# The second gate of a hybrid block: three of four pairs of output units as seven half-width block products

## The chip, the cores and the metric

The kernel runs on one core of a Trainium2 chip, as one launch. The metric is the device time of that launch in microseconds (us); the times given are medians of runs, and one further execution was recorded by the hardware profiler. TensorE is called PE below (PEld is its weight load), VectorE DVE, ScalarE ACT, GpSimd POOL and SyncE SP. SP and POOL here issue the DMAs: SP plain ones, POOL those that add to what the destination holds.

## The reference, cut to what matters

One decoder block on 512 tokens of 1024 channels, in float32. `h` is the normalised, shifted and scaled input. The part around the change is the merge of two branches by two sigmoid gates:

```python
proj = h @ w_in
z, xbc, dt_raw, u_pool, gate_logits = jnp.split(proj, IN_SPLITS, axis=-1)
...
y_ssd = y.reshape(b, seq, D_INNER) @ w_branch_ssd
y_pool = causal_multiscale_pool(u_pool, pool_w, pool_scale) @ w_branch_pool
g_ssd, g_pool = jnp.split(jax.nn.sigmoid(gate_logits), N_BRANCHES, axis=-1)
return (g_ssd * y_ssd + g_pool * y_pool) @ w_out
```

The gate of the SSD branch, `g_ssd`, is the "second gate": a 512 x 1024 by 1024 x 1024 product, then a sigmoid. The block ends with an MLP of width 4096 with a squared ReLU and a last norm.

## The kernel before, in words

All activations are kept transposed: channels on the 128 partitions, the 512 tokens along the free axis. A matrix product is cut into **units** of 128 output channels: `unit` (line 160) takes a packed weight of 128 x 1024 (eight blocks of 128 x 128, one for each 128 input channels) and accumulates into one PSUM bank of 128 x 512. To keep float32 accuracy, each operand is held as a rounded high part and a low rest, and `mm3` (line 154) issues three matmuls for each block: high by high, high by low, low by high. So a unit is 8 x 3 = 24 matmuls of 512 columns.

`load_unit` (line 136) brings the weight into one of four raw buffers (`RAW`) by a DMA on SP, rounds it on ACT (line 146), and takes the rest on DVE (line 147) into two of the `HL` buffers. `split` (line 123) does the same with an activation (lines 126 and 127). Buffers come from `Slots`, a first-in-first-out list of tiles: a tile's next user waits for all readers of its last one. `ada` (line 168) loads a row of the modulation weights into a raw buffer as well and reduces it on DVE (line 172); 32 of these rows are spread over the middle of the kernel by `ada_next`. The instructions of each engine are put in order by the framework when the program is built, by priority and its own estimate of when each is ready; work can be placed well ahead of its position in the program.

The order of the middle of the kernel is: four SSD groups with their fillers; eight units of the gate of the pooling branch (`wgate[8 + j]`, line 700); inside it, after the fourth, the last part of the SSD branch product (`bs`) and a mix of the pool; eight units of the pool projection (`wbp`, line 718), which multiply into `merged` (line 720), with two `ada` each; the eight units of the second gate (`wgate[j]`, line 725): sigmoid on ACT (line 728), times the SSD branch `acc` (line 730), plus `merged` (line 731), and `split`, giving `mg`; then the output projection (`wout`, line 784), whose every unit reads all eight `mg`. The second gate also issues the last four `ada`.

The MLP already uses another form, for **pairs** of output units (class `Pair`, line 877). The contraction's eight blocks are taken as four even-odd couples, the pair's two units and the two halves of the tokens are the other two splits, so that the product is a 2 x 2 by 2 x 2 block product, done with seven block products in place of eight (Winograd's form of Strassen's scheme). `product` (line 871) is one of these: four blocks by three matmuls of 256 columns, so a pair is 7 x 12 = 84 matmuls of 256 columns. The sums it needs:

- of the moving operand, `sums` (line 841): four operations of 256 columns on DVE for each of four couples, and two splits (`two`, line 835);
- of the weights, S1 to S4 beside A11, A12 and A22: two by accumulating DMAs on POOL (lines 892 and 894), two by DVE (lines 908 and 919), and the splits by `keep` (lines 896 to 901, with the rounding and the rest at lines 837 and 839);
- of the products: two copies on ACT (lines 961 and 968), two additions on DVE (lines 973 and 980).

`run_jobs` (line 996) runs a list of jobs, pairs or plain ones: it fetches the weights of those ahead as raw buffers come free (`pump`), prepares the next job between the products of the present one, and leaves the last two products of a pair to the time of the next job, so that PE does not wait for DVE:

```python
self.mul(self.ac[:, :H], "A11", "B11", True)   # first
self.mul(self.c12, "S1", "T1", True)           # open
self.mul(self.ac[:, :H], "S2", "T2")           # middle
self.mul(self.c11, "A12", "B21")
self.mul(self.ac[:, :H], "S3", "T3")           # third
self.mul(self.c12, "S4", "B22")                # close
self.mul(self.ac[:, :H], "A22", "T4")          # finish
```

PSUM has eight banks of 128 x 512: a pair uses a set of two of banks 4 to 7 (`BE`), and one of banks 0 and 1 (`AC`); banks 2 and 3 are left for plain units.

Of the kernel before, what the change touches and what calls it, by code (L numbers as in the profile page):

```python
# [12 lines left out]
P = 128  # L13
# [49 lines left out]
def block_kernel(tc, xp, crow, arow, par, adaT, wstart, wz, wx, wpool_in, wgate, wpw, wbs, wbp, wout, wup, wdn, out):  # L63
# [3 lines left out]
    with (  # L67
# [616 lines left out]

        urgent[0] = True
# [6 lines left out]
        PADS = slots("pad", 9, (P, T + 16))  # L692
        pu = [pool_in(gi, t) for gi in range(4) for t in range(2)]
        rest = run(3, after(2, pu[:6] + [pool_mix(0)] + pu[6:]))
        later = [p_.get() for p_ in (XS, SZ, XS)]
        F = Slots(lambda i, dt: later[i // 4][:, i % 4, :], 12)


        merged = []
        for j in range(8):  # L700
# [5 lines left out]
            if j == 1:  # L706
                for _ in rest:
                    pass
                later.append(SZ.get())
                F.free += range(12, 16)  # L710
                PU.free += PS.free
            ada_next()
            if j == 3:
# [3 lines left out]
                pool_mix(1)()  # L717
        for j in range(8):
# [3 lines left out]
            ada_next(2)  # L722
        free(pout)
        mg = []
        for j in range(8):
            gs = F.get()
            ps = unit(wgate[j], h)
            last = act.activation(gs, ps, AF.Sigmoid)
            PU.put(ps)
            dve.tensor_tensor(gs, gs, acc[j], ALU.mult)  # L730
            dve.tensor_tensor(gs, gs, merged[j], ALU.add)
            S.put(acc[j])
            F.put(merged[j])
            mg.append(split(gs))
            F.put(gs)
            if rows:
                ada_next()
# [90 lines left out]
        HL = Slots(lambda i, dt: D(B0 + i if i < 8 else B0 + 9, dt, 48), 9)  # L828
# [4 lines left out]
        Y4S = Slots(lambda i, dt: slots("pad", 1, (P, T + 16), first=APART[i][0]).get(dt)[:, APART[i][1]:APART[i][1] + T], 4)  # L833

        def two(src, dst, late=None):

            act.copy(dst[0], src)  # L837
            with tc.issue_after(late.ins) if late else nullcontext():
                dve.tensor_tensor(dst[1], src, dst[0].bitcast(F32), ALU.subtract)  # L839

        def sums(u1, u2, ts):

            dve.tensor_tensor(u1[:, :H], u1[:, :H], u1[:, H:], ALU.subtract)
            dve.tensor_tensor(u1[:, H:], u2[:, H:], u1[:, H:], ALU.subtract)
# [32 lines left out]
        class Pair:  # L877
# [79 lines left out]
            def open(self):  # L957
                self.take()
                self.mul(self.c12, "S1", "T1", True)
                with tc.high_priority():  # L960
                    act.copy(self.s5, self.c12)
# [370 lines left out]
```

## Time and profile before

| what | value |
|---|---|
| median of three runs | 957.82 us (955.89 to 960.07) |
| the profiled execution | 958.36 us |
| its span, first to last instruction | 956.6 us |
| mean granted clock of PE over the span | 0.995 |
| matmul groups of 512 columns, three products (lines 156 to 158) | 920 each, of these 112 with 256 columns (operands `s` and `d`) |
| half-width matmuls of pairs (line 875) | 1848, in 22 pairs |

A row of the busy time by stretch reads: the stretch in us from the start of the span, its length, and then for each engine the us in which it was busy and the number of instructions. In a timeline a row reads: start, duration, engine, line, operation, the tiles written and read, the shape, a count, and in brackets how long the engine stood idle before it and what released it. Matmuls are pipelined: their durations overlap, and what one costs is the spacing of their starts.

### The profile page before, as it was taken

What the parts mean: (1) busy time and instruction counts of PE and PEld (TensorE: products, weight loads), DVE (VectorE), ACT (ScalarE), POOL (GpSimd) and SP (SyncE); (2) the same over time, 40 slices, a digit from 0 to 9 for tenths busy, and PEclk for the clock granted to TensorE, in tenths of its full rate; (3) what the DMA queues carried; (4) which work ended last, traced back from release to release, by engine and by line L of the source; (5) the groups of instructions that cost most, each with busy time, mean ns of one, the idle gap of its engine ahead of it and who ended that gap; (6) DMA issues with size and microseconds to landing.
All of it is one profiled execution on the core that took longest, in us unless ns stands there. A gap on an engine that the chain in (4) does not pass through costs nothing.

```text
span 956.6 us, 14343 instructions
## 1 busy us (share of the span) xinstructions
PE 940.4 (98%) x5491; PEld 810.9 (85%) x5491; DVE 721.3 (75%) x1120; ACT 540.8 (57%) x891; POOL 124.3 (13%) x131
## 2 busy tenths in 40 slices
PE   8999999999999999999999999999999999999996
PEld 4877888888888888787888888998999899899986
DVE  7978868566767776987568565698869888977973
ACT  5479976568436642553421343486458547646753
POOL 0102320220312031410000000001111111111000
PEclk9999999999999999999999999999999999999998
DMA  9836343433354343464578464035676676677412
GB/s 362 310 119 181 118 129 98 136 121 97 88 144 122 99 116 96 158 192 156 181 237 287 152 201 151 29 91 126 159 200 152 151 198 147 165 194 169 133 35 88
DMA packets 70503, 145.55 MB, mean 152 GB/s; under 512 B 5473, under 2 KB 30305, under 8 KB 70434
## 3 DMA queue, kind: packets, MB, share of 16 engines
q1 hardware_dynamic: 64672, 134.14, 44.5%
q0 software_dynamic: 5760, 10.49, 7.4%
q8 instruction: 43, 0.70, 0.3%
q14 instruction: 26, 0.21, 0.1%
q10 hardware_dynamic: 2, 0.00, 0.0%
HBM read 142.39 MB, written 2.23 MB: 151 GB/s over the span
## 4 chain that ended last, share of the span: by engine, by line
PE 75%; DVE 12%; DMA 5%; ACT 4%; issue 2%; POOL 0%; SPq 0%; DVEq 0%; POOLq 0%; ACTq 0%
PE ps L875 18%; PE ps L156 16%; PE ps L157 16%; PE ps L158 16%; PE ps L328 4%; DMA d<-wdn 3%; DVE d L839 2%; DVE d L147 1%; PE ps L549 1%; DMA d<-cs_d 1%; DVE s L127 1%; DVE s L839 1%; ACT d L837 1%; PE ps L529 1%; DMA d<-wstart 1%
## 5 line engine op out<-in xcount | busy, mean ns | idle before, releaser
L156 PE MATMUL ps<-s,d 128*128 128x512 f32 (+1 forms) x920 | 350.6, 381 | 1.1 <-ACT s L649 0.6
L157 PE MATMUL ps<-s,d 128*128 128x512 f32 (+1 forms) x920 | 345.9, 376 | 0.2 <-DVE s L127 0.2
L158 PE MATMUL ps<-s,d 128*128 128x512 f32 (+1 forms) x920 | 346.0, 376 | 0.0
L156 PEld LDWEIGHTS ps<-s,d 128*128 128x128 f32 x920 | 172.6, 188 | 35.7 <-issue 2.1
L158 PEld LDWEIGHTS ps<-s,d 128*128 128x128 f32 x920 | 172.8, 188 | 32.4 <-issue 0.2
L157 PEld LDWEIGHTS ps<-s,d 128*128 128x128 f32 x920 | 172.8, 188 | 31.2 <-DVE s L127 0.7
L875 PE MATMUL ps<-s,d 128*128 128x256 f32 x1314 | 162.2, 279 | 2.1 <-DVE d L839 2.0
L875 PEld LDWEIGHTS ps<-s,d 128*128 128x128 f32 x1314 | 156.9, 188 | 4.2 <-DVE d L839 3.8
L147 DVE TENSOR_TENSOR d<-d,d 128x1024 fp32r<-128x1024 f32 x88 | 112.6, 1280 | 63.1 <-ACT d L146 56.6
L146 ACT CAST d<-d 128x1024 fp32r<-128x1024 f32 x88 | 92.0, 1046 | 117.8 <-PE ps L157 77.2
L837 ACT CAST d<-d 128x1024 fp32r<-128x1024 f32 x86 | 89.8, 1048 | 56.9 <-DVE d L919 24.1
L839 DVE TENSOR_TENSOR d<-d,d 128x1024 fp32r<-128x1024 f32 x86 | 104.7, 1221 | 18.9 <-ACT d L837 10.2
L172 DVE CUSTOM_DVE_ANT_0 d<-d,d,par_t 128x1024 f32<-128x1024 f32 x32 | 41.8, 1306 | 27.3 <-DMA d<-adaT 27.1
L892 POOL DMA_DIRECT2D d<-wdn x10 | 8.8, 884 | 307.5 <-DMA d<-wdn 258.7
L328 PE MATMUL ps<-s,d 128*128 128x512 f32 x168 | 41.7, 403 | 1.9 <-ACT s L316 1.9
L499 ACT ACTIVATE d<-d,ncs 128x128 f32<-128x128 f32 x128 | 39.9, 390 | 3.9 <-POOL d L495 3.8
L328 PEld LDWEIGHTS ps<-s,d 128*128 128x128 f32 x168 | 32.5, 194 | 10.0 <-ACT s L316 2.4
L397 DVE SCALAR_TENSOR_TENSOR s<-ps,par_t,s 128x511 f32<-128x511 f32 (+2 forms) x54 | 39.6, 741 | 0.3
L126 ACT CAST s<-s 128x512 fp32r<-128x512 f32 x32 | 19.7, 619 | 31.1 <-POOL s L511 18.7
L495 POOL TENSOR_SCALAR_AFFINE_SELECT d<-d 128x1024 f32<-128x1024 f32 x16 | 18.2, 1137 | 90.8 <-ACT cd L492 37.0
L127 DVE TENSOR_TENSOR s<-s,s 128x512 fp32r<-128x512 f32 x32 | 25.7, 805 | 4.4 <-ACT s L126 4.3
L511 POOL TENSOR_TENSOR s<-s,dec 128x512 f32<-128x512 f32 x12 | 15.8, 1313 | 90.7 <-issue 56.4
(231 smaller groups left out, 1231.6 us busy)
## 6 DMA issues: line engine op xcount, KB each, us to landing
d<-adaT SPq DMA_DIRECT2D x32, 512.0 KB, 4.2
d<-wup SPq DMA_DIRECT2D x32, 512.0 KB, 4.8
d<-wdn SPq DMA_DIRECT2D x32, 512.0 KB, 4.6
d<-wx SPq DMA_DIRECT2D x18, 512.0 KB, 3.6
d<-cs_d SPq DMA_DIRECT2D x16, 512.0 KB, 6.0
d<-wbs SPq DMA_DIRECT2D x16, 512.0 KB, 3.6
d<-wgate SPq DMA_DIRECT2D x16, 512.0 KB, 4.2
d<-wz SPq DMA_DIRECT2D x15, 512.0 KB, 3.6
```

Of the source, the lines that this page charges most:

```text
L146: act.copy(hi[:, :w], r[:, a:a + w])
L147: (low or dve).tensor_tensor(lo[:, :w], r[:, a:a + w], hi[:, :w].bitcast(F32), ALU.subtract)
L156: pe.matmul(ps, whi, xhi[:, t0:t1], start=start, stop=False)
L157: pe.matmul(ps, whi, xlo[:, t0:t1], start=False, stop=False)
L158: pe.matmul(ps, wlo, xhi[:, t0:t1], start=False, stop=stop)
L172: dve.tensor_tensor_reduce(r, r, cbc, 1.0, col("b_ada", j), ALU.mult, ALU.add, mod[:, j:j + 1])
L328: pe.matmul(first[u], w[u][i // 2], h[k][i % 2], start=k == 0 and i == 0, stop=k == 7 and i == 2)
L397: dve.scalar_tensor_tensor(t[:, sh:], ps[:, :T - sh], w(3 - sh), t[:, sh:], ALU.mult, ALU.add)
L499: act.activation(m[:, i, :], m[:, i, :], AF.Exp, bias=ncs[:, c, g * HG + i:g * HG + i + 1])
L837: act.copy(dst[0], src)
L839: dve.tensor_tensor(dst[1], src, dst[0].bitcast(F32), ALU.subtract)
L875: pe.matmul(ps, x, y, start=start and m == 0 and i == 0, stop=m == 3 and i == 2, skip_group_check=True)
```

## The change

The second gate's first six units become three pairs; its last two stay plain units.

- The weights are packed once more, as pairs (`wgs`).
- `whole(m)` restores the float32 values of two couples' blocks of `h` by adding its two parts on DVE, makes the four sums T1 to T4 of them and splits these. It is called at the last two units of the pooling gate and at units 1 and 3 of `wbp`. The sums of the first two couples lie where gate buffers of the merge were, those of the other two in eight `S` slots.
- `gate_pair` applies the sigmoid to the pair's results and calls `merge`, the old sequence of product, sum and split.
- Classes and helpers of the MLP's pairs move ahead of the gate stage, unchanged but for their buffers: in the gate stage, the pairs' raw buffers are `RAW`, their splits come from `HL`, which is eleven buffers long by then (eight before).
- The first pair is fetched and wholly prepared at unit 4 of `wbp`; `run_jobs` becomes a generator that stops there and goes on after `wbp`. The fetches of the other two pairs stand behind the last `wbp` unit in the program.
- The last four `ada` are issued by the two plain units (two each) in place of the first four units of the gate.
- In the gate stage plain units have PSUM banks 2 and 3 only.

```diff
+        def whole(m):
+
+            us = [S.get(), S.get()]
+            for u, (hi, lo) in zip(us, h[2 * m:2 * m + 2]):
+                dve.tensor_tensor(u, hi.bitcast(F32), lo.bitcast(F32), ALU.add)
+            if m < 2:
+                ts = [tuple(later[2 + m][:, 2 * i + a, :].bitcast(F32R) for a in range(2)) for i in range(2)]
+            else:
+                ts = [(S.get(F32R), S.get(F32R)) for _ in range(2)]
+            sums(*us, ts)
+            S.put(*us)
+            return ts
+
+        def merge(j, gs):
+
+            dve.tensor_tensor(gs, gs, acc[j], ALU.mult)
+            dve.tensor_tensor(gs, gs, merged[j], ALU.add)
+            S.put(acc[j])
+            F.put(merged[j])
+            mg.append(split(gs))
+            S.put(gs)
+
+        def gate_pair(p):
+
+            def f(i, ps, sign):
+                gs = S.get()
+                n = T // len(ps)
+                for i_, part in enumerate(ps):
+                    act.activation(gs[:, n * i_:n * (i_ + 1)], part, AF.Sigmoid, scale=float(sign))
+                merge(2 * p + i, gs)
+            return Pair(wgs[p], hb, f)
...
+            def run(self, between):
+                for j in range(2 * NPAIR, 8):
+                    ps = unit(wgate[j], h)
+                    if between:
+                        between()
+                        between = None
+                    gs = S.get()
+                    self.last = act.activation(gs, ps, AF.Sigmoid)
+                    PU.put(ps)
+                    merge(j, gs)
+                    while len(rows) > 2 * (7 - j):
+                        ada_next()
...
+            if j > 5:
+                ht.append(whole(j - 6))
+        mg, hb = [], {}
+        for j in range(8):
+            ps = unit(wbp[j], pout)
+            dve.tensor_tensor(merged[j], merged[j], ps, ALU.mult)
+            PU.put(ps)
+            ada_next(2)
+            if j in (1, 3):
+                ht.append(whole(len(ht)))
+            if j == 4:
...
+                RL, Z = RAW, HL
+                HP = Slots(lambda i, dt: D(NRAW + i, dt, 48), 11)
+                HP.free = HL.free
+                hb.update(moving(h, ht))
+                gates = [gate_pair(p) for p in range(NPAIR)] + [GateUnits()]
+                steps = run_jobs(gates)
+                next(steps)
+        free(pout)
+        banks, BE, AC = banks_of_pairs()
+        PU.free = [2, 3]
+        for _ in steps:
+            pass
```

In `run_jobs`, ahead of the loop over the jobs:

```diff
-            pump()
-            jobs[0].prepare()
+            if isinstance(jobs[0], Pair):
+                todo.pop(0).fetch()
+                jobs[0].prepare()
+                jobs[0].prepare_more()
+                jobs[0].prepare_rest()
+            else:
+                pump()
+                jobs[0].prepare()
+            yield
             pump()
```

More of the change, by code (lines that the diff above doesn't have):

```diff
@@ L60, in put, with block_kernel @@
             self.free.append(self.owner.pop(id(t))[0])
-def block_kernel(tc, xp, crow, arow, par, adaT, wstart, wz, wx, wpool_in, wgate, wpw, wbs, wbp, wout, wup, wdn, out):
+def block_kernel(tc, xp, crow, arow, par, adaT, wstart, wz, wx, wpool_in, wgate, wgs, wpw, wbs, wbp, wout, wup, wdn, out):
     nc = tc.nc
@@ L683, in run, with two, sums @@
             return steps
+        mids = []
+        def two(src, dst, late=None):
+            act.copy(dst[0], src)
+            with tc.issue_after(late.ins) if late else nullcontext():
+                dve.tensor_tensor(dst[1], src, dst[0].bitcast(F32), ALU.subtract)
+        def sums(u1, u2, ts):
+            dve.tensor_tensor(u1[:, :H], u1[:, :H], u1[:, H:], ALU.subtract)
+            dve.tensor_tensor(u1[:, H:], u2[:, H:], u1[:, H:], ALU.subtract)
+            dve.scalar_tensor_tensor(u2[:, H:], u2[:, H:], -1.0, u1[:, :H], ALU.mult, ALU.subtract)
+            dve.scalar_tensor_tensor(u2[:, :H], u2[:, H:], -1.0, u2[:, :H], ALU.mult, ALU.subtract)
+            for u, t in zip((u1, u2), ts):
+                if len(t) == 2:
+                    two(u, t)
+                else:
+                    two(u[:, :H], t[:2])
+                    two(u[:, H:], t[2:])
@@ L709, in block_kernel @@
                 later.append(SZ.get())
[L710 removed]
+                HL.free += range(8, 11)
                 PU.free += PS.free
@@ L722, in block_kernel @@
             ada_next(2)
-        free(pout)
[L724 to L737, printed above, removed]
+            if j in (1, 3):
+                ht.append(whole(len(ht)))
+            if j == 4:
+                Y4 = Slots(lambda i, dt: slots("pad", 1, (P, T + 16), first=OTHER[3 + i]).get(dt)[:, :T], 2)
+                s5_t = slots("pad", 1, (P, T + 16), first=OTHER[2]).get()[:, :T]
+                U5 = Slots(lambda i, dt: s5_t[:, i * H:(i + 1) * H], 2)
+                RL, Z = RAW, HL
[5 more added lines that the diff above has]
+                next(steps)
+        free(pout)
+        banks, BE, AC = banks_of_pairs()
+        PU.free = [2, 3]
+        for _ in steps:
+            pass
+        free([t for m in ht[2:] for t in m])
+        PU.free = [2, 3, 0, 1, 4, 5, 6, 7]
+        last = gates[-1].last
         gated = done[1]
@@ L832, in block_kernel @@
         ut = [[[raws[p][:, 2 * i + k, :].bitcast(F32R) for k in range(2)] for i in range(2)] for p in range(2)]
[L833 to L844, printed above, removed]
-            dve.scalar_tensor_tensor(u2[:, H:], u2[:, H:], -1.0, u1[:, :H], ALU.mult, ALU.subtract)
-            dve.scalar_tensor_tensor(u2[:, :H], u2[:, H:], -1.0, u2[:, :H], ALU.mult, ALU.subtract)
-            for u, t in zip((u1, u2), ts):
-                if len(t) == 2:
-                    two(u, t)
-                else:
-                    two(u[:, :H], t[:2])
-                    two(u[:, H:], t[2:])
```

354 lines of the change are left out of this document (182 added, 172 removed).

## The prediction

> **What bounds the kernel now.** I read the head of the page first, then its chain.
>
> ```profile
> span 956.6 us, 14343 instructions
> ...
> PE 940.4 (98%) x5491; PEld 810.9 (85%) x5491; DVE 721.3 (75%) x1120; ACT 540.8 (57%) x891; POOL 124.3 (13%) x131
> ...
> PE 75%; DVE 12%; DMA 5%; ACT 4%; issue 2%; POOL 0%; SPq 0%; DVEq 0%; POOLq 0%; ACTq 0%
> ```
>
> TensorE (PE) is busy for 940.4 of 956.6 us. The chain gives 25% to other engines, but that alone does not mean that PE stood still there, so I next took the busy times by stretch: the end of the gates of the pooling branch, the pool projection (`wbp`), the second gate (the changed stage), the output projection, and one stretch of the MLP. Columns are the stretch, its length, busy time and count of PE, PEld, DVE, ACT and POOL, granted clock, DMA share, GB/s.
>
> ```profile
> 466.00:484.50 18.50, 18.50 (x84) 15.30 (x83) 8.74 (x13) 6.05 (x8) 0.00 (x0) 1.00 0.51 161
> 484.50:527.60 43.10, 43.10 (x192) 35.69 (x191) 32.07 (x51) 7.51 (x8) 0.00 (x0) 1.00 0.79 264
> 527.60:571.20 43.60, 43.60 (x194) 36.12 (x193) 25.44 (x32) 18.22 (x26) 0.00 (x0) 1.00 0.54 180
> 571.20:605.00 33.80, 33.80 (x179) 28.81 (x178) 19.55 (x26) 13.35 (x20) 0.00 (x0) 1.00 0.41 130
> ...
> 724.00:754.00 30.00, 29.86 (x206) 27.39 (x205) 28.44 (x49) 23.45 (x41) 3.47 (x4) 1.00 0.65 162
> ```
>
> PE never idles from 466 to 605 us, at full granted clock. So the second gate is worth what its matmuls cost PE, and there is no idle time of PE in it to win back. Next come its waits, and the price of a matmul as PE really spaces them. The rows are: a PE wait (total, times, longest); two weight splits of the second gate, five units apart; two copies of the same product, two MLP pairs apart.
>
> ```profile
> PE ps L875 <- DVE d L839: 2.0, 5, 0.6
> ```
> ```profile
> 538.61 1.22 DVE L147 TENSOR_TENSOR d<-d,d 128x1024 fp32r<-128x1024 f32 x1 [1.55 <-ACT d L146]
> ...
> 565.81 1.22 DVE L147 TENSOR_TENSOR d<-d,d 128x1024 fp32r<-128x1024 f32 x1 [1.50 <-ACT d L146]
> ```
> ```profile
> 690.15 0.37 ACT L961 COPY pad<-ps 128x256 f32<-128x256 f32 x1 [0.77 <-PE ps L875]
> ...
> 709.94 0.38 ACT L961 COPY pad<-ps 128x256 f32<-128x256 f32 x1 [0.49 <-PE ps L875]
> ```
>
> A plain unit takes (565.81 - 538.61)/5 = 5.440 us for 24 matmuls of 512 columns: 226.7 ns each. A pair takes (709.94 - 690.15)/2 = 9.895 us for 84 matmuls of 256: 117.8 ns each. This is 4% over half of 226.7, and it eats a third of the eighth that seven products save over eight.
>
> **The change part by part.**
>
> *Removed and added on PE.* Six of eight plain units go: 6 x 5.440 = 32.64 us. Three pairs come: 3 x 9.895 = 29.69 us. The difference is **-2.96 us**, all on the path, since PE is the bound before and after. The stage shrinks from 43.5 to 40.6 us.
>
> *Added on DVE.* Spacing of starts in a dense stretch gives the prices:
>
> ```profile
> 659.83 0.68 DVE L919 TENSOR_TENSOR d<-d,d 128x512 f32<-128x512 f32 x1
> 660.43 0.68 DVE L839 TENSOR_TENSOR sz<-s,sz 128x512 fp32r<-128x512 f32 x1
> 661.04 0.41 DVE L844 TENSOR_TENSOR pad<-pad,pad 128x256 f32<-128x256 f32 x1
> 661.37 1.22 DVE L839 TENSOR_TENSOR d<-d,d 128x1024 fp32r<-128x1024 f32 x1
> 662.51 0.41 DVE L845 SCALAR_TENSOR_TENSOR pad<-pad,pad 128x256 f32<-128x256 f32 x1
> ```
>
> These are 0.60 us for 512 columns, 0.33 for 256, 1.14 for 1024. One `whole(m)` is two adds, four half-width sums and two splits: 4 x 0.60 + 4 x 0.33 = 3.7 us, four times 15 us. Preparing one pair is three splits of 1024 and three operations of 512: 5.2 us, and its two additions after products 2 and 3 are 0.7 us; the two plain units in its place cost 2.3 us of splits. The merge is the same six operations per pair as before.
>
> By stage, with the first and last of those splits, the last `ada` row, and the last use of a `wbp` product, which marks the border of the two stages:
>
> ```profile
> 516.59 1.22 DVE L147 TENSOR_TENSOR d<-d,d 128x1024 fp32r<-128x1024 f32 x1
> ...
> 524.30 1.28 DVE L172 CUSTOM_DVE_ANT_0 d<-d,d,par_t 128x1024 f32<-128x1024 f32 x1
> ...
> 526.31 1.22 DVE L147 TENSOR_TENSOR d<-d,d 128x1024 fp32r<-128x1024 f32 x1
> 527.44 0.68 DVE L720 TENSOR_TENSOR sz<-sz,ps 128x512 f32<-128x512 f32 x1
> ```
>
> From 466 to 484.5 us DVE has 18.5 - 8.7 = 9.8 us free, and `whole(0)` and `whole(1)` (7.5) fit. In the `wbp` stage it was busy for 32.1 of 43.1; the change adds two `whole` (7.5), pair 0 (5.2) and the first part of pair 1 (1.7), and takes away three early gate splits (3 x 1.14 = 3.4) and the four `ada` rows that the second gate used to issue and that were done ahead, the last at 524.3 (4 x 1.28 = 5.1): 38.0 of 43.1, or 88%. In the gate stage it was 25.4; six unit splits go (6.8), two preparations (10.4), three pairs' additions (2.0) and the four `ada` (5.1) come: 36.1 of 40.6, or 89%. Cover: the last window above has DVE at 28.44 of 30.00 beside pairs and plain units, with PE still at 29.86. I therefore take the DVE work as hidden in the middle of both stages. If the cover fails, PE waits for a split; the PE wait row above is that case, 0.4 us a time. ACT gains two casts per `whole` and a few casts and copies per pair, from 7.5 and 18.2 us of 43, and stays hidden.
>
> *Added on the DMA queues.* Rows: the two queues; a load to landing; the accumulating issue of line 892 on POOL (its 884 ns), and its landing.
>
> ```profile
> q1 hardware_dynamic: 64672, 134.14, 44.5%
> q0 software_dynamic: 5760, 10.49, 7.4%
> ```
> ```profile
> d<-wgate SPq DMA_DIRECT2D x16, 512.0 KB, 4.2
> ```
> ```profile
> L892 POOL DMA_DIRECT2D d<-wdn x10 | 8.8, 884 | 307.5 <-DMA d<-wdn 258.7
> ```
> ```profile
> DMA to landing us min/median/max: 4.0/4.6/7.0
> ```
>
> By share of the span, a plain megabyte costs 0.445 x 956.6/134.14 = 3.2 us of all engines, an accumulated one 0.074 x 956.6/10.49 = 6.7. A pair moves 1.25 MB plain and 0.5 MB accumulated: 7.4 us against 3.2 for two units. In the gate stage the engines were busy for 0.54 x 43.6 = 23.5 us. Without four unit loads (-6.3), with pair 2 and most of pair 1 (+14.8), units 6 and 7 (+3.2) and four `ada` (+6.3) they would be busy for 41 us, all of the stage. What slips is last in the program's order: the loads of `wout` and of x, and the next stage has its DMA engines free for 59%. Cost taken: none; if a `wout` load itself came late, PE would stand as in rival 1.
>
> *Added waits.* (a) Pair 0's entry. What is queued behind it on SP and POOL are `wbp` loads 5 to 7 and the fetches of pairs 1 and 2, which share the four raw buffers; PE waits for their splits. I take one wait of 0.4 us. (b) The end of the stage, rows below: ACT, DVE, PE.
>
> ```profile
> 572.16 0.59 ACT L728 ACTIVATE sz<-ps 128x512 f32<-128x512 f32 x1
> ...
> 575.05 0.62 ACT L126 CAST s<-sz 128x512 fp32r<-128x512 f32 x1 [0.99 <-DVE sz L731]
> ```
> ```profile
> 573.60 0.69 DVE L730 TENSOR_TENSOR sz<-sz,s 128x512 f32<-128x512 f32 x1
> 574.32 0.69 DVE L731 TENSOR_TENSOR sz<-sz,sz 128x512 f32<-128x512 f32 x1
> 575.70 0.69 DVE L127 TENSOR_TENSOR s<-sz,s 128x512 fp32r<-128x512 f32 x1 [0.69 <-ACT s L126]
> ```
> ```profile
> 570.83 0.39 PE L156 MATMUL ps<-s,d 128*128 128x512 f32 x1
> ...
> 575.36 0.39 PE L158 MATMUL ps<-s,d 128*128 128x512 f32 x1
> 575.72 0.72 PE L156 MATMUL ps<-s,d 128*128 128x512 f32 x2
> ```
>
> `wout` unit 0 starts at 570.83 and can run 21 matmuls (4.76 us) before it needs the last merged pair, whose rounded half is written until 575.67: PE started it at 575.72. The slack is already nil, so whatever stands in front of the last merge is paid in full. I add 0.2 us.
>
> *Sum.* -2.96 + 0.4 + 0.2 = -2.4 us. The profiled execution took 958.36 us (span 956.6 and 1.8 around it), so 956.0 on its footing; it lies 0.5 us above the median of 957.82, so **955.5 us** as a median. The waits are bounded by 0 below (PE has no idle to give back, so the stage cannot gain more than 2.96) and by the rivals above.
>
> **One rule against the row.** The spacing rows give 117.8/226.7 = 0.52. The Trainium skill, "TensorE: Matmul & The Clock Gate", section "Back-to-back issue gap", says that in a stream of weight load and matmul the spacing is set by both, and gives 81 ns at 128 columns and 131 at 512. By an estimate along a line between those figures, 256 columns cost 98 ns, a pair 8.2 us against 6.3 for two units, and the change would lose 5.8 us. The trace disagrees: 226.7 ns, not 131.
>
> **Rivals.**
>
> 1. *The tail is late.* Four `ada` rows now stand in the program beside the last two units, DVE and DMA are nearly full, and DVE runs in order. If two `ada` (2.6 us) and the merge of unit 6 (2.1 us) stand before the last merge, PE waits up to 4.7 us: 957.8 - 3.0 + 4.7 = 959.5. For: nil slack, the 89%. Against: in the old kernel all `ada` were done ahead of their place, by the row at 524.30.
>
> 2. *The raw buffers become the bound (slower).*
>
> ```profile
> 490.94 3.45 SPq L141 DMA_DIRECT2D d<-wbp  x2
> ...
> 503.47 0.33 SPq L141 DMA_DIRECT2D d<-wbp  x1
> ```
> ```profile
> 508.48 1.05 ACT L146 CAST d<-d 128x1024 fp32r<-128x1024 f32 x1 [8.02 <-DMA d<-wbp]
> ```
>
> The `wbp` stage already had its loads late at the cast. Pair 0 now holds two of the four buffers for a load (4.2), an issue and an accumulation (0.9 + 4.6) and its DVE work (5.2): from about 491 to 505.8. `wbp` unit 6 takes one of them: load 4.2, cast 1.1, so ready at 511.1, and PE needs it two units before 527.6, at 516.7. The margin is 5.6 us; two `whole` (7.5) and the `ada` queued between can eat it, and pair 1 comes out of the same ring. From the point where DVE adds over 5.6 us to the ring, every further one is PE idle. With both `whole` (7.5), four `ada` (5.1) and 1 us of latency in it, 13.6 - 5.6 = 8 us of stall: 957.8 - 3.0 + 8 = 963. Against: the margin, and the later `ada`.
>
> 3. *Halving the width saves less here.* Break-even is 48 x 226.7/84 = 129.5 ns. If the price followed the duration of a matmul rather than its spacing,
>
> ```profile
> L158 PE MATMUL ps<-s,d 128*128 128x512 f32 x808 | 315.0, 390 | 0.0
> ...
> L875 PE MATMUL ps<-s,d 128*128 128x256 f32 x1314 | 162.2, 279 | 2.1 <-DVE d L839 2.0
> ```
>
> it would be 279/390 x 226.7 = 162 ns, 2.7 us more per pair: 966. The 9.895 us period speaks against it. The rule of the Trainium skill above would end on this side too.
>
> That the change does not do what it says has no room: the matmul counts are fixed by the program.
>
> **How the numbers follow.** Forecast 0.56, tail 0.26, raw buffers 0.16, width 0.02. Runs of this kernel spread by 2 us either way, and about 0.5% (4.8 us) is what a measurement of it can tell from no change: below 953.0 is faster, above 962.6 slower. Faster: 0.04, from the forecast's scatter alone, since the whole gain is 0.3%. Slower: 0.12 from the buffers and 0.02 from the width, 0.14. Same: 0.82. The range starts at no wait at all, 954.9, less 1.5 of scatter: 953.4; it ends at 962.0, over the whole tail case and the near part of the buffers.
>
> **What would show it.** 252 half-width matmuls in the stage, 9.9 us from pair to pair and PE busy throughout: the forecast. PE idle at the first matmul on merged unit 7, released by DVE or ACT: rival 1. PE idle between 510 and 545 us, released by a weight split behind DMA: rival 2. Spacing well over 118 ns without idle: rival 3. I am wrong altogether if the gain passes 4 us, or if a stage after the output projection, which I take as merely shifted, changes its length.

## The result, and the profile after

The changed kernel takes **973.54 us** (median of 4 runs, 971.08 to 976.87) against 958.08 for the kernel before in the same session: ratio 1.0163, 95% interval 1.0141 to 1.0184. It is slower by 1.6%. Forecast were 955.5 us and a range that ended at 962.0.

The head of the page and its chain, of the kernel after:

```profile
span 970.7 us, 14658 instructions
...
PE 942.7 (97%) x5599; PEld 815.7 (84%) x5599; DVE 745.4 (77%) x1170; ACT 552.6 (57%) x914; POOL 130.2 (13%) x137
...
PE 72%; DVE 10%; DMA 8%; ACT 5%; issue 4%; POOL 0%; SPq 0%; DVEq 0%; POOLq 0%; ACTq 0%
```

The shares hardly move: DVE goes from 75% to 77% of the span, and DMA from 5% to 8% of the chain. What happened stands in the busy times by stretch. First the kernel before, then the kernel after (columns as in the prediction: stretch, length, busy time and count of PE, PEld, DVE, ACT and POOL, granted clock, DMA share, GB/s):

```profile
430.00:440.00 10.00, 9.77 (x42) 7.59 (x41) 7.39 (x10) 7.07 (x10) 0.00 (x0) 1.00 0.31 85
510.00:520.00 10.00, 10.00 (x46) 8.29 (x45) 7.38 (x10) 2.11 (x2) 0.00 (x0) 1.00 0.85 265
520.00:530.00 10.00, 10.00 (x45) 8.28 (x45) 7.10 (x12) 1.85 (x2) 0.00 (x0) 1.00 0.88 305
...
580.00:590.00 10.00, 10.00 (x46) 8.29 (x45) 5.42 (x7) 4.32 (x5) 0.00 (x0) 1.00 0.58 173
```
```profile
430.00:440.00 10.00, 7.76 (x24) 4.70 (x23) 8.36 (x12) 8.69 (x12) 0.00 (x0) 0.83 0.33 108
510.00:520.00 10.00, 8.61 (x37) 6.51 (x36) 5.28 (x10) 3.04 (x3) 0.86 (x1) 1.00 0.74 214
520.00:530.00 10.00, 7.26 (x26) 5.57 (x26) 6.47 (x9) 0.00 (x0) 0.00 (x0) 0.83 0.43 131
540.00:550.00 10.00, 9.00 (x79) 8.80 (x78) 6.07 (x9) 5.74 (x10) 0.00 (x0) 1.00 0.30 80
560.00:570.00 10.00, 8.30 (x58) 7.51 (x57) 9.44 (x14) 5.26 (x9) 0.00 (x0) 1.00 0.83 269
580.00:590.00 10.00, 7.49 (x30) 5.65 (x29) 7.46 (x11) 6.57 (x9) 0.00 (x0) 0.92 0.87 295
```

Count matmuls here, not busy time: a matmul that starts late or runs at a lower clock also counts as busy. Where all are 512 columns wide, each one that is missing is 0.2267 us. There are four losses:

- **A**, 430 to 440 us: 18 fewer, 4.1 us. This lies a hundred microseconds ahead of the changed stage.
- **B**, 510 to 530 us, `wbp` units 5 to 7: 28 fewer, 6.4 us.
- **C**, in the pairs: PE idle for 1.0 and 1.7 us, 2.7 us.
- **D**, 580 to 590 us, `wout` unit 0: 16 fewer, 3.6 us.

That is 16.8 us lost; less the 2.96 that the products were to save, 13.8 us remain, and the spans differ by 970.7 - 956.6 = 14.1. The rest of the kernel is merely shifted: from the first squared-ReLU activation to the end it is 318.8 us before and 319.7 after. That the two figures meet so closely is partly luck: the count leaves out some four matmuls of D behind 590 us (42 from 590 to 600 us, where 46 fit), and the products save less than 2.96 (below).

**A.** ACT in its order, in the timeline of the kernel after and then of the kernel before (start, duration, engine, line, operation, tiles, shape; in brackets the idle time ahead and what ended it):

```profile
425.33 1.05 ACT L146 CAST d<-d 128x1024 fp32r<-128x1024 f32 x1 [1.59 <-DMA d<-wbs]
...
428.19 0.69 ACT L589 ACTIVATE s<-ps,eps_t 128x512 f32<-128x512 f32 x1
428.77 0.61 ACT L689 CAST pad<-pad 128x512 fp32r<-128x512 f32 x1
```
```profile
426.52 0.69 ACT L589 ACTIVATE s<-ps,eps_t 128x512 f32<-128x512 f32 x1
```

Line 589 is the norm of the last SSD group, for which PE waits through several steps. In the new kernel a weight cast for the `bs` product, which waited 1.59 us for its DMA, stands ahead of it, and right behind it a split of the quarter A22 for a pair (line 689) that PE needs over 100 us later. The cast could be put there because the list of split buffers has eleven entries, three more, from that place on. The split of A22 goes into buffers of its own (`Y4S`); nothing in the program held it back.

**B.** The same view of the kernel after, around the late `wbp` units: ACT, then SP's issues, then DVE:

```profile
512.30 2.00 ACT L146 CAST d<-d 128x1024 fp32r<-128x1024 f32 x2 [5.82 <-DMA d<-wbp]
517.21 1.05 ACT L146 CAST d<-d 128x1024 fp32r<-128x1024 f32 x1 [2.91 <-DMA d<-wbp]
```
```profile
491.80 0.34 SPq L141 DMA_DIRECT2D d<-wbp  x1
493.34 12.61 SPq L171 DMA_DIRECT2D d<-adaT  x3
508.57 0.33 SPq L141 DMA_DIRECT2D d<-wbp  x1
...
513.49 0.33 SPq L141 DMA_DIRECT2D d<-wbp  x1
```
```profile
500.32 0.69 DVE L755 TENSOR_TENSOR d<-d 128x512 f32<-128x512 f32 x1 [5.14 <-DMA d<-wgs]
...
512.25 1.22 DVE L691 TENSOR_TENSOR d<-d,d 128x1024 fp32r<-128x1024 f32 x1
...
521.60 1.28 DVE L172 CUSTOM_DVE_ANT_0 d<-d,d,par_t 128x1024 f32<-128x1024 f32 x1 [6.05 <-DMA d<-adaT]
...
522.82 1.22 DVE L147 TENSOR_TENSOR d<-d,d 128x1024 fp32r<-128x1024 f32 x1
```

Unit 5 was issued at 491.80 and unit 7 at 508.57; unit 6, whose raw buffer was one of pair 0's, followed at 513.49. In the 17 us between the first two, SP issued three `ada` loads and took 12.61 us for them, each waiting for a raw buffer. Then ACT cast units 7 and 5 together at 512.30: the cast of unit 7 stood first in its order, so unit 5 waited for a load issued 17 us after its own. Unit 6 was cast at 517.21, but its rest on DVE stood behind an `ada` reduction that itself waited for a DMA for 6.05 us. PE waited 2.74 us for it. Unit 6's cast had ended at 518.26, before PE stopped (its last start was at 520.96), so this wait came from the order on DVE. The first two rows of DVE show why unit 6 was loaded so late: pair 0's preparation ran from 500.32 to 513.47, with three `ada` reductions among it, and its last split was the last reader of the raw buffer that unit 6 got at 513.49. The Trainium skill, "Perfetto Trace Analysis", section "Tensor Engine Instruction (MATMUL, LD_WEIGHTS)", says of ACT and DVE that they are strict first-in-first-out; these rows agree.

**C and D.** The additions between pairs (ACT, DVE, PE), then the last merge (DVE, PE), again of the kernel after:

```profile
541.49 1.05 ACT L689 CAST d<-d 128x1024 fp32r<-128x1024 f32 x1 [3.55 <-DMA d<-wgs]
```
```profile
542.57 1.22 DVE L691 TENSOR_TENSOR d<-d,d 128x1024 fp32r<-128x1024 f32 x1 [5.71 <-ACT d L689]
543.72 0.42 DVE L820 TENSOR_TENSOR ps<-ps,pad 128x256 f32<-128x256 f32 x1
...
584.41 1.29 DVE L147 TENSOR_TENSOR s<-d,s 128x512 fp32r<-128x512 f32 x2 [1.60 <-ACT s L146]
585.62 0.68 DVE L936 TENSOR_TENSOR s<-s,sz 128x512 f32<-128x512 f32 x1
```
```profile
544.20 0.61 PE L722 MATMUL ps<-xs,d 128*128 128x256 f32 x3 [1.00 <-DVE ps L820]
...
563.85 0.62 PE L722 MATMUL ps<-xs,d 128*128 128x256 f32 x3 [1.70 <-DVE ps L820]
...
587.01 0.50 PE L156 MATMUL ps<-s,d 128*128 128x512 f32 x1 [2.51 <-ACT s L126]
```

C's first wait and D have one pattern. The addition of line 820 takes 0.42 us and frees the bank that PE wants; it stood behind the next pair's weight split, and DVE waited 5.71 us for that. The last merge (line 936) stood behind splits of `wout` units 5 to 7, whose load was late, and PE waited 2.51 us. C's second wait, of 1.70 us, is different: the addition stood behind two multiplications of the merge (562.16 to 563.36 us), and DVE was not at a standstill but busy for 9.44 us of the 10 from 560 on.

### The profile page after: what moved, and what is told of

Read it like the earlier page. It is cut to its first block, busy times and chain, and to the rows that moved or that the text cites. A ratio compares the mean times of both kernels' runs of the same rounds, so it can differ in the third digit from the quotient of the medians.

```text
span 970.7 us, 14658 instructions
## 1 busy us (share of the span) xinstructions
PE 942.7 (97%) x5599; PEld 815.7 (84%) x5599; DVE 745.4 (77%) x1170; ACT 552.6 (57%) x914; POOL 130.2 (13%) x137
## 4 chain that ended last, share of the span: by engine, by line
PE 72%; DVE 10%; DMA 8%; ACT 5%; issue 4%; POOL 0%; SPq 0%; DVEq 0%; POOLq 0%; ACTq 0%
PE ps L156 16%; PE ps L722 16%; PE ps L157 16%; PE ps L158 16%; PE ps L328 4%; DMA d<-wdn 2%; DVE d L147 1%; PE ps L549 1%; DVE d L691 1%; DMA d<-wup 1%; DMA d<-wgs 1%; DMA d<-wout 1%; ACT d L689 1%; DMA d<-adaT 1%; ACT d L146 1%
## 5 line engine op out<-in xcount | busy, mean ns | idle before, releaser
L156 PE MATMUL ps<-s,d 128*128 128x512 f32 (+1 forms) x872 | 333.4, 383 | 5.1 <-ACT s L126 3.0
L158 PE MATMUL ps<-s,d 128*128 128x512 f32 (+1 forms) x872 | 329.9, 379 | 3.3 <-DVE d L147 3.3
L157 PE MATMUL ps<-s,d 128*128 128x512 f32 (+1 forms) x872 | 329.4, 378 | 1.7 <-DVE s L127 1.7
L722 PE MATMUL ps<-s,d 128*128 128x256 f32 x1476 | 182.6, 279 | 2.5 <-DVE d L691 2.2
L689 ACT CAST d<-d 128x1024 fp32r<-128x1024 f32 x95 | 99.2, 1049 | 88.5 <-DVE d L766 28.2
L147 DVE TENSOR_TENSOR d<-d,d 128x1024 fp32r<-128x1024 f32 x82 | 106.2, 1296 | 51.9 <-ACT d L146 44.5
L691 DVE TENSOR_TENSOR d<-d,d 128x1024 fp32r<-128x1024 f32 x95 | 115.4, 1219 | 24.1 <-ACT d L689 17.0
L146 ACT CAST d<-d 128x1024 fp32r<-128x1024 f32 x82 | 85.5, 1045 | 76.0 <-PE ps L157 29.0
L172 DVE CUSTOM_DVE_ANT_0 d<-d,d,par_t 128x1024 f32<-128x1024 f32 x32 | 40.9, 1278 | 13.8 <-DMA d<-adaT 13.7
L126 ACT CAST s<-s 128x512 fp32r<-128x512 f32 x40 | 24.6, 619 | 37.5 <-POOL s L511 18.7
L127 DVE TENSOR_TENSOR s<-s,s 128x512 fp32r<-128x512 f32 x40 | 31.0, 779 | 4.4 <-ACT s L126 4.3
L689 ACT CAST s<-s 128x512 fp32r<-128x512 f32 (+1 forms) x42 | 22.1, 537 | 17.0 <-DVE s L696 8.2
L722 PE MATMUL ps<-sz,d 128*128 128x256 f32 x207 | 30.6, 279 | 0.0
```

Source lines behind the costliest of these rows:

```text
L146: act.copy(hi[:, :w], r[:, a:a + w])
L147: (low or dve).tensor_tensor(lo[:, :w], r[:, a:a + w], hi[:, :w].bitcast(F32), ALU.subtract)
L156: pe.matmul(ps, whi, xhi[:, t0:t1], start=start, stop=False)
L157: pe.matmul(ps, whi, xlo[:, t0:t1], start=False, stop=False)
L158: pe.matmul(ps, wlo, xhi[:, t0:t1], start=False, stop=stop)
L172: dve.tensor_tensor_reduce(r, r, cbc, 1.0, col("b_ada", j), ALU.mult, ALU.add, mod[:, j:j + 1])
```

## The experiments

The theory after this reading: the DVE and PE arithmetic was about right, and the time went because **work for later, placed early on an engine that runs in order, waits for a late load with urgent work behind it**. Pair 0, in the ring of four raw buffers, makes the loads late. The rival: DVE simply has too much to do. All times below are medians, each ratio is to runs of the kernel before in the same session.

| run | edit | us | ratio (95%) |
|---|---|---|---|
| after | the change | 973.54 | 1.0163 (1.0141 to 1.0184) |
| no_pairs | eight plain units, sums kept | 961.28 | 1.0049 (1.0027 to 1.0071) |
| one_pair | one pair | 966.05 | 1.0091 (1.0067 to 1.0115) |
| hl_a22 | mends A | 973.5 | 1.0165 (1.0131 to 1.0199) |
| wbp_chain | splits of `wbp` in program order | 974.11 | 1.0167 (1.0120 to 1.0215) |
| tail_hold | mends D | 971.14 | 1.0138 (1.0112 to 1.0164) |
| three | these three together | 968.58 | 1.0101 (1.0080 to 1.0122) |
| mid | three, and C | 967.78 | 1.0101 (1.0078 to 1.0124) |
| no_whole | the change without the sums' DVE work | 971.05 | 1.0146 (1.0124 to 1.0168) |
| first6 | mid, plain unit 6 ahead of the pairs | 964.70 | 1.0076 (1.0047 to 1.0105) |
| first6_a | first6, two more placements | 957.43 | 1.0000 (0.9987 to 1.0012) |
| no_pairs_b | no_pairs, A and D mended | 956.68 | 0.9990 (0.9974 to 1.0007) |
| first6_c | first6_a, last `ada` moved | 956.42 | 0.9982 (0.9969 to 0.9995) |

### Without the pairs, and with one

```diff
-        NPAIR = 3
+        NPAIR = 0
```

> All eight gate units are multiplied whole again (NPAIR = 0). What stays of the change: the sums of h's quarters (four times `whole`, about 15 us of VectorE work), the deeper list of split buffers (11 in place of 8), the gate's units in the pair stage's PSUM list. Theory 'order in the queues' (an early planned instruction that waits for a late DMA holds up what stands behind it, and the pairs bring the late DMAs): the wait at the wbp units 5 to 7 is gone or under 1 us, what the deeper buffers cost at 430 to 440 us stays (about 4 us), time 958 to 963. Rival 'load' (VectorE simply has too much to do in the wbp stage): the sums alone make PE wait 3 us or more between 490 and 530 us, time 963 or more.

It took 961.28 us. The stretches of this run:

```profile
430.00:440.00 10.00, 7.49 (x31) 5.34 (x30) 8.46 (x11) 8.98 (x12) 0.00 (x0) 1.00 0.34 111
510.00:520.00 10.00, 10.00 (x46) 8.29 (x45) 5.77 (x11) 3.77 (x4) 0.00 (x0) 1.00 0.70 224
520.00:530.00 10.00, 10.00 (x46) 8.29 (x45) 3.31 (x4) 1.48 (x2) 0.00 (x0) 1.00 0.31 107
570.00:580.00 10.00, 7.99 (x36) 6.27 (x34) 7.69 (x11) 6.70 (x10) 0.00 (x0) 1.00 0.50 152
```

A and D are there without a single pair (31 and 36 matmuls); B is not (46 and 46). So A and D come from what surrounds the pairs, B from the pairs. The profiled execution took 967.12 us, the longest of ten, so these rows show more than the 3.3 us that the median lost.

> The changed kernel with one pair of units by seven half-width products and six plain units. Pair 0 is fetched at the same place in the wbp stage; pairs 1 and 2 are gone, so no addition between pairs and fewer accumulating DMAs. Theory: the loss before the stage (about 4 us at 430 to 440) and that of the wbp units (5 to 7 us from 510 to 530) both stay, since pair 0 alone causes the second; that between pairs goes: time 966 to 970, though two pairs fewer save only 2 us less on PE. Rival: each pair brings its own loss in like measure, a third of the way from the run without pairs (961.3) to the changed kernel (973.5): about 965 or less.

With `NPAIR = 1` the time is 966.05, at the lower end of the theory and 1 us above the rival's bound, which does not tell them apart. The count does: it is 27 from 510 to 520 us and 46 from 520 to 530, so 18 matmuls (4.1 us) are lost in B: one pair in the ring brings most of B.

### Each loss mended alone

Run hl_a22, A:

```diff
-                HL.free += range(8, 11)
...
                 pool_mix(1)()
+                HL.free += range(8, 11)
...
-                two(self.y4, hl)
+                with tc.issue_after(hold[0].ins):
+                    two(self.y4, hl)
```

`hold[0]` is the last sigmoid of the pooling branch's gate.

> The changed kernel with two placements altered: the three further split buffers join the list only after pool_mix(1) in place of before the bs loads, and the splits of the A22 quarter of pairs 0 and 1 are held behind the last sigmoid of the pooling branch's gate. Theory: the loss at 430 to 440 us (24 matmuls in that stretch, 42 before) comes from these early splits on ScalarE and VectorE ahead of the last group's normalisation; the stretch goes back to 40 to 43 matmuls, the time falls by 3.5 to 4.5 us to about 969.5, and the wbp stage and the tail keep their waits. Rival: the loss comes from elsewhere (DMA load, or the clock), and the stretch keeps under 30 matmuls; time unchanged within 1 us.

The cause of A is right: 42 matmuls again from 430 to 440 us. The time did not fall: 973.5. What A gave back was lost in B (39 matmuls missing from 510 to 530 us, 28 in the changed kernel) and in D (22 from 580 to 590 us, 30 there). The rows are two stretches, PE's one long wait in B, and the cast that ended it:

```profile
430.00:440.00 10.00, 9.77 (x42) 7.53 (x41) 6.76 (x9) 7.08 (x9) 0.00 (x0) 1.00 0.37 105
...
510.00:520.00 10.00, 4.30 (x9) 2.99 (x10) 5.37 (x14) 3.04 (x3) 0.86 (x1) 0.72 0.75 232
```
```profile
515.66 0.80 PE L156 MATMUL ps<-s,d 128*128 128x512 f32 x1 [5.79 <-ACT d L146]
```
```profile
513.62 1.99 ACT L146 CAST d<-d 128x1024 fp32r<-128x1024 f32 x2 [7.40 <-DMA d<-wbp]
```

PE came to the `wbp` units earlier, and the loads did not: the wait grew from 0.86 us (at 514.35 in the changed kernel) to 5.79, and ended 1.3 us later. The cast that PE waited for is the second of the two, again unit 5's, whose load was issued at 492.44; ahead of it stood the cast of a load issued at 508.97, against 508.57 in the changed kernel. So the ring of raw buffers sets when that load comes, however early PE is, and the order on ACT makes unit 5 wait for it. Theory and rival both missed this; while B stands, mending A is worth nothing.

Run wbp_chain, part of B (the rests are chained in the same way):

```diff
+                    with tc.issue_after(old[0].ins) if old and old[0] else nullcontext():
+                        c_ = act.copy(hi[:, :w], r[:, a:a + w])
```

> The changed kernel with the splits of the wbp units held to program order on ScalarE and on VectorE (each cast behind the cast before it, each remainder behind the remainder before it), so that unit 5, which landed at about 496 us, no longer waits behind unit 7, which landed at 512.3. Loads and DMA order stay. Theory 'order in the queues': the waits at 514 to 516 us (0.86 and 0.53) go, unit 6 still lands late, so 2 to 3 us of the 6.6 lost from 510 to 530 come back: time about 971. Theory 'raw buffers' (the ring of four alone sets it): unit 6 is as late as before, and PE merely waits elsewhere: time unchanged within 1 us.

974.11 us: by its number the second theory held. With unit 5 ahead of unit 7 on ACT, the first wait is one of 1.0 us at 516.85, and at 525.39 PE waited 2.8 us for unit 6 as before. The ring is not shown as the reason, though, since both waits were for the order on DVE. Unit 5's cast had ended at 510.82; its rest came at 515.58, behind an `ada` reduction and pair 0's last split. Unit 6's rest (524.12), with its cast done by 521.3, stood again behind an `ada` reduction that waited for its load:

```profile
522.91 1.28 DVE L177 CUSTOM_DVE_ANT_0 d<-d,d,par_t 128x1024 f32<-128x1024 f32 x1 [6.12 <-DMA d<-adaT]
```

To mend the order of the units' splits among themselves is not enough; what else stands between them on DVE counts as well.

Run tail_hold, D:

```diff
-        w = [load_unit(wout[j], at=S, cols=T) for j in (5, 6, 7)]
+        with tc.issue_after(gated.ins), tc.issue_after(merged_last.ins):
+            w = [load_unit(wout[j], at=S, cols=T) for j in (5, 6, 7)]
```

> The changed kernel with the splits of wout units 5 to 7 held behind the last merge of the second gate on ScalarE and VectorE. Theory: the 30 matmuls in the stretch from 580 to 590 us come from those splits standing, for a late load, ahead of the last merge; the stretch goes back to over 40 matmuls and the time falls by 2.5 to 3.5 us to about 970.5. Rival: the last merge is late of itself (its sigmoid or VectorE's load), the wait at the first product on merged unit 7 stays over 2 us and the time is unchanged within 1 us.

971.14 us, 2.4 less, just under what was expected, and 44 matmuls from 580 to 590 us. The ranges of the two runs overlap (968.93 to 973.25 against 971.08 to 976.87); the stretch, and that no wait of PE at the last merge is left, show the cause of D.

### Together, and the additions

> The three placements of the earlier runs together: late split buffers and late A22 splits (loss at 430 to 440 us), wbp splits in program order (unit 5), wout splits behind the last merge (tail). Pair 0 still takes two of the four raw buffers in the middle of the wbp stage. Theory 'queue order alone': the three losses of about 4, 2 to 3 and 3 us all go, and with the additions between pairs (3 us) left the time is about 962. Theory 'raw buffers': reaching the wbp units 5 to 7 earlier only makes PE wait longer there for loads whose time the ring of four sets (as the run without the early A22 splits did, 5.8 us in one wait); 4 to 7 us are lost between 500 and 530 us and the time is 965 to 969.

968.58 us, in the second theory's range; 27 and 45 matmuls from 510 to 530 us, 19 lost. The three holds are worth 5 us together; B still costs 4.3, and D is partly back (32 matmuls from 580 to 590 us). The second theory's reason does not fit: PE's wait in B, 2.35 us at 513.40, was for unit 5's rest on DVE at 512.13, and unit 5's cast had ended at 506.02. In between DVE worked without a gap over 0.15 us, on two of pair 0's splits and two `ada` reductions among others.

Run mid: `job.middle()` is recorded ahead of `ahead()` in the gate's pairs, and `keep` and the first sum of `prepare` hold DVE's part behind `mids[-1]` there too.

> The kernel of the run 'three', with VectorE's part of the next pair's first splits held behind the present pair's addition that frees PE's accumulator (the middle addition is recorded before the next pair is prepared, and the remainder's subtraction waits for it). Theory: the waits of the products on that addition (2.9 us in three waits in the changed kernel) go to under 0.5 us, and the time falls by 2 to 3 us against 'three'. Rival: VectorE is too full between 550 and 570 us, the wait moves to the next pair's splits, and the time is within 1 us of 'three'.

967.78 us, within 1 us of three: by its number the rival. In the pairs the wait on the addition fell from 2.4 to 1.0 us, and one of 0.75 us on the next pair's split came in its place. So the wait moved in part, as the rival had it. The rest of the gain went elsewhere in the profiled execution, the longest of four (970.51): 4.1 us in one wait for unit 5's rest, and 3.8 us at the last merge, where this split stood ahead on DVE:

```profile
582.06 1.23 DVE L150 TENSOR_TENSOR d<-d,d 128x1024 fp32r<-128x1024 f32 x1 [1.62 <-ACT d L148]
```

By its width of 1024 it is a split of one of the `wout` units 0 to 4, which are not held; its cast waited 1.98 us for its load. This is D's pattern again.

### Is it DVE's load?

```diff
-            sums(*us, ts)
-            S.put(*us)
+            for t, x in zip(ts, h[2 * m:2 * m + 2]):
+                for a in range(2):
+                    act.copy(t[a], x[a].bitcast(F32))
```

The copies stand in for the sums and their splits, so the pairs' products are computed from other values; their number and shape stay.

> The changed kernel without the sums of h's quarters: the four `whole` steps write copies of h on ScalarE where VectorE made the weight sums' partners (six additions and two splits each, about 15 us of VectorE work in all, left out). All products, loads and accumulating DMAs stay. Theory 'order and ring': PE still loses 4 us or more from 510 to 530 us, since what is late there are loads and what is queued behind them; time 970 to 974. Rival 'load' (VectorE's extra work is what makes the ring late, the rival of the prediction that added both `whole` into it): the loss from 510 to 530 us falls under 2 us and the time to 968 or less.

This split the theories. Stretches of the run:

```profile
510.00:520.00 10.00, 9.47 (x40) 7.20 (x40) 3.81 (x6) 3.05 (x3) 0.25 (x1) 1.00 0.51 145
520.00:530.00 10.00, 9.69 (x43) 7.70 (x42) 8.04 (x11) 1.05 (x1) 0.49 (x1) 1.00 0.69 213
```

8 matmuls lost in B instead of 28, 1.8 us: just what the load theory asked for. But the time is 971.05, which the order theory gave: B gave back 4.5 us by the count, the total 2.5, and the rest turns up at other waits: one of 2.6 us on the addition of line 820, ended at 541.34, where the changed kernel has 1.0; 21 matmuls from 430 to 440 us, where it has 24; and 26 from 580 to 590, where it has 30. So DVE's work does lengthen the round of a raw buffer, as the prediction's second rival had it (the second of the loads of units 6 and 7 was issued by 510.78, in place of 513.49); but taking it away does not make the kernel fast, and with the same work but no pairs (no_pairs) nothing is lost in B. It takes the two together, the sums and pair 0. Pair 0 brings its hold of half of the ring and its own work on DVE ahead of the units' splits, and no run takes away one of these alone.

### Pair 0 out of the ring

The order becomes unit 6, three pairs, unit 7; no pair is fetched until the last `wbp` load is in the program, and until unit 6 has run a pair is fetched only if two raw buffers stay free beside its own.

```diff
-                gates = [gate_pair(p) for p in range(NPAIR)] + [GateUnits()]
+                gates = [GateUnits([6])] + [gate_pair(p) for p in range(NPAIR)] + [GateUnits([7])]
...
-                next(steps)
+        next(steps)
```

> The kernel of the run 'mid', with the order of the second gate changed: plain unit 6, the three pairs, plain unit 7, so that pair 0 is fetched behind the last wbp load and no longer holds raw buffers in the wbp stage; its matmuls are the same. Theory 'raw buffers': the wbp stage runs without a wait as in the kernel before (45 to 46 matmuls in each stretch of 10 us up to 530), and with the other three losses mended the time is 955 to 958, the -2.96 of the halved products showing at least in part. Theory 'queue order alone' (the ring is no limit): no change against 'mid'. Rival 'load': VectorE and the DMA engines have too much in both stages whatever the order, and 3 us or more of waits stay between 500 and 600 us: time 960 or more.

964.70 us, 3 less, where "raw buffers" had promised 955 to 958; by its number the rival "load" held. Up to 520 us the stage now runs whole (45 matmuls from 510 to 520), and the waits moved: PE stood 1.7 us for a bank that a `wbp` product frees, which was behind an `ada` reduction on DVE, and 3.8 us for the copy of line 821, behind this on ACT:

```profile
536.19 1.04 ACT L694 CAST d<-d 128x1024 fp32r<-128x1024 f32 x1 [15.96 <-DMA d<-wgs]
537.14 0.59 ACT L987 ACTIVATE s<-ps 128x512 f32<-128x512 f32 x1
537.63 0.38 ACT L821 COPY ps<-ps 128x256 f32<-128x256 f32 x1
```

The cast of pair 1's weights kept ACT at a standstill for 16 us, ahead of the sigmoid of a unit that PE had finished and of the copy that PE waited for. This is the pattern of D and of most of B and C, so the next run held that cast back and moved two `ada` loads:

```diff
-            act.copy(dst[0], src)
+            with tc.issue_after(first.ins) if first else nullcontext():
+                act.copy(dst[0], src)
...
-                    while len(rows) > 2 * (7 - j):
+                    while j == 7 and rows:
```

> The kernel of the run 'first6' with two more placements: the ada loads that plain unit 6 issued go to unit 7, and ScalarE's casts of the next pair's splits wait behind the present pair's copy of its first sum, so that a late weight load no longer stands before the copy and the sigmoid that free PE's banks (in 'first6' ScalarE stood 16 us there with PE waiting 3.8 us, and the product of wbp unit 7 stood behind an ada reduction, 1.7 us). Theory (order of instructions behind late loads): these 5.5 us and the clock drop after them go; time 957 to 960, equal to the kernel before or up to 2 us faster. Rival 'load': pair 1's weights are late of themselves, PE waits at its first product instead, and the time stays at 962 or more.

**957.43 us**, ratio 1.0000 (0.9987 to 1.0012): the theory. The whole loss is gone with every sum, product and accumulating DMA still there; only the order and the time at which buffers are given out differ. Which of the two edits did more is not shown: with the `ada` loads moved, the second issue of a pair's first weight tile comes at 507.34 us, in place of 523.26, so the cast that is held may not have been late any more. A stretch, and the first half-width product and the second matmul of unit 7 in PE's timeline:

```profile
550.00:560.00 10.00, 10.00 (x85) 9.84 (x84) 9.85 (x14) 6.68 (x10) 0.00 (x0) 1.00 0.79 255
```
```profile
529.71 0.52 PE L728 MATMUL ps<-s,d 128*128 128x256 f32 x3
...
560.33 0.40 PE L162 MATMUL ps<-s,d 128*128 128x512 f32 x1
```

The three pairs take 560.33 - 0.23 - 529.71 = 30.39 us (the 0.23 are for unit 7's first matmul, which lies among them), 120.6 ns a matmul; with two units of 5.44 the stage is 41.3 us, 2.2 under the 43.5 of eight plain units. DVE is busy for 9.85 of 10 us from 550 to 560, and PE does not stop: here a full DVE is covered.

### Two last runs

> The kernel of the run 'no_pairs' (sums of h's quarters, eight plain units) with the further split buffers given late and the wout splits behind the last merge, as in the runs that placed these. Theory: what the run without pairs lost (961.3 against 958.0) came from these two placements, at 430 to 440 and at 570 to 590 us, and the 15 us of sums on VectorE are hidden: 957.5 to 959, equal to the kernel before. Rival: the sums cost something of themselves: 960 or more.

956.68 us, 0.8 below the theory's range and equal to the kernel before by its interval: the sums on DVE are hidden, and all that the run without pairs lost was A and D.

> The kernel of the run 'first6_a' with its last four ada loads moved from unit 7 of the second gate to the first units of wout, since two of their reductions stood on VectorE between the last merges and PE waited 0.6 us at the first product on the last merged unit. Theory: that wait goes, time 0.5 to 1 us under first6_a, about 956.7. Rival: the ada loads now share the raw buffers with the wout loads, and a wout unit is late by 1 us or more: 958 or more.

956.42 us, the time of the theory. Its profiled execution, the longest of twelve (959.47), shows neither the theory nor the rival: PE waited 1.8 us at 572.59 for the rest of a merged unit on DVE, which stood behind an `ada` reduction and two splits of `wout` units (568.37 to 571.85 us). The median is 1 us under first6_a, about the spread of the runs, and as low as no_pairs_b, which has no pairs. So it is 0.2% under the kernel before by its interval, but that the pairs make any of this is not shown.

The profiles say more than the medians in one place. From the first sigmoid of the pooling branch's gate to the first squared-ReLU activation, the profiled executions take 217.6 us before, 230.9 after, 217.6 in no_pairs_b, 216.1 in first6_a and 218.1 in first6_c. So first6_a kept 1.5 of the 2.2 us up to the MLP, and then took 322.1 us to the end against 318.8 before. These are single executions; whether the longer end has to do with the change is not shown.

## Why the prediction was wrong, point by point

- **What bounds the kernel**: right. PE had no idle time there, and a wait added was paid in full, some of them with a lower clock on top (last section).
- **The product term, -2.96 us**: right in mechanism, a little large. The stage saves 2.2 us where nothing stops it: 30.39 us for three pairs against 29.69. (In the working, 4% over half costs a pair 3.4 of the 12.5 points that seven products save, so rather over a quarter than a third.)
- **"I therefore take the DVE work as hidden in the middle of both stages"**: this is the step that failed. It weighed shares of a stage, 88% and 89%, and left 0.6 us for waits in the sum; by the count, 16.8 were lost. The amount was harmless with another order (first6_a, no_pairs_b). What cost time was which instruction stood in front: in D, in the first wait of C and in most of B, a short, urgent instruction on DVE or ACT stood behind an early one that waited for a DMA. Only C's second wait, 1.7 us, was behind DVE's work itself.
- **The DMA queues, "Cost taken: none"**: wrong for the same reason. The DMA engines' share was not the limit (0.74 and 0.43 from 510 to 530 us); the raw buffers held the loads back, with 12.61 us for three issues. (The terms given for the gate stage add up to 41.5 us, not 41.)
- **Pair 0's entry, 0.4 us**: the mis-sized term. It was priced as one wait for a late split. What pair 0 did was to hold a raw buffer until 513.47 us and to put its splits ahead of the units' on DVE: 6.4 us in B.
- **Rival 2, raw buffers, 0.16**: right in its place (510 to 530 us), in its releaser (a weight split behind DMA) and in size (8 us expected, 6.4 lost), and far too unlikely. The margin of 5.6 us that spoke against it was eaten by pair 0's work on DVE, as the rival feared: it was to end at 505.8 us and ended at 513.47, with three `ada` reductions among it. What the rival did not have is the order: PE waited for unit 5, whose load had been issued at 491.80, and for a rest that stood behind an `ada` reduction.
- **Rival 1, the tail, 0.26**: it came about as well (3.6 us against up to 4.7), but through the splits of `wout`, not through `ada` rows. It was weighed as an alternative to rival 2. Both come from the order on DVE and ACT, and both came.
- **Ahead of the stage**: nothing. The longer list of split buffers was described as part of the change, and not asked what could start earlier because of it. That is A: no section looked at 430 us.
- **Rival 3, half-width price, 0.02**: rightly dismissed. The measured 120.6 ns lies under the break-even of 129.5. The rule of the Trainium skill, "TensorE: Matmul & The Clock Gate", section "Back-to-back issue gap", by which the pairs would lose by themselves, does not hold here.

What stays open: how B divides between the sums, pair 0's own work on DVE and its two raw buffers, since first6 moves the last two together; which of first6_a's two placements did more; and whether 1 or 2 us of the pairs' 2.2 can be kept in the total.

## What to carry to other kernels

In a kernel that is full on its main engine, check an added piece of work by asking for each queue what stands behind it while it waits for its load, and not only whether the engine has room; if work can start earlier because buffers were added, look at what it then stands in front of. Keep pieces with a long hold (a pair: load, add, split) out of a short ring that feeds the stage running now, and mend waits that hang on the same late loads together, since one of them mended alone can merely move the wait.

## What was not expected of the hardware

Some waits of PE cost more than their length. After the 2.74 us wait of B in the changed kernel, PE's timeline reads:

```profile
524.09 0.80 PE L158 MATMUL ps<-s,d 128*128 128x512 f32 x1 [2.74 <-DVE d L147]
524.68 0.63 PE L156 MATMUL ps<-s,d 128*128 128x512 f32 x1
525.11 0.63 PE L157 MATMUL ps<-s,d 128*128 128x512 f32 x1
...
527.11 0.39 PE L156 MATMUL ps<-s,d 128*128 128x512 f32 x1
```

From 524.68 to 526.82 the spacing is 0.43 us, where it is 0.227 elsewhere; the granted clock of that stretch is 0.83. From 524.09 to 527.11 PE starts seven matmuls, which take 1.6 us at the usual spacing and took 3.0: 1.4 us on top of 2.7. After the 5.79 us of hl_a22 the clock of its stretch is 0.72. The waits of 0.9 and 0.5 us at 514 and 516 us are followed by the usual spacing. The length of a wait does not decide it. The rows are from A in the changed kernel, and from D in wbp_chain:

```profile
434.56 0.64 PE L157 MATMUL ps<-s,d 128*128 128x512 f32 x1 [1.22 <-DVE s L127]
435.00 0.63 PE L158 MATMUL ps<-s,d 128*128 128x512 f32 x1
```
```profile
588.49 0.50 PE L161 MATMUL ps<-s,d 128*128 128x512 f32 x1 [2.93 <-ACT s L126]
```

In A, after waits of 0.52 and 1.22 us with one matmul between them, PE runs at a spacing of 0.43 us and more up to 438.16, which is 1.8 of A's 4.1 us. After the 2.93 us of wbp_chain the spacing is 0.24 us from 588.83 on, and the granted clock 1.00. The rivals' prices left this out. The Trainium skill, "TensorE: Matmul & The Clock Gate", section "What's actually happening", says that the clock falls to half after an idle window of about 3.4 us; the halved rate agrees, but here a gap of 2.74 us was enough, and so was one of 1.22 us soon after one of 0.52, while one of 2.93 us was not followed by it.
